# A two-layer encoder on one Trainium2 core: the middle of the first output projection as four seven-product units, and the recurrent unit in twelve turns

## The chip, the core and the metric

The kernel runs on one core of a Trainium2 chip. The metric is the device time of one execution in microseconds; the time given for a kernel is the median of its runs. The profile is of one more execution, taken with the hardware profiler. Engines carry the names of the profile: PE (TensorE), DVE (VectorE), ACT (ScalarE), POOL (GpSimd), SP (the queue that issues most transfers).

## What is computed

An encoder of two layers on 512 tokens of 2048 features, in 32-bit floats. The first layer is attention (8 query heads, 2 key heads) beside a gated linear recurrent unit of 1024 features; the second is a chunked matrix-memory recurrence. Cut to the part that the change touches, the first layer is

```
hn   = rmsnorm(x, gain)
proj = hn @ w_in                       # q, k, v, g_attn, x_lru, g_lru
attn = softmax attention of q, k, v
xc   = conv4(x_lru) + conv_b
r, i = sigmoid(xc @ wa + ba), sigmoid(xc @ wx + bx)
a    = exp(8 * r * log_sigmoid(lam))
u    = sqrt(1 - a*a) * (i * xc)
y    = scan(h = a*h + u) forward + the same backward
mix  = [attn * silu(g_attn), y * silu(g_lru)]
x    = x + mix @ w_out                 # the first output projection
```

and the second layer begins with `rmsnorm(x) @ w_in2`.

## The kernel before

**Matmuls.** Every product of two 32-bit matrices is three matmuls (`mm3`, L170; issued on L157): each operand is split into a high part (a cast on ACT, L153) and a low part (a subtraction on DVE, L154), and high by low, high by high and low by high are summed in PSUM. Activations lie with features on the partitions, 256 features (a "chunk") to a tile, so a product over 2048 features has eight steps.

**Groups and units.** The work of TensorE is a list of groups, built at the end of `build` and run by `run_steps` (L298). A plain group makes 512 output features in 8 steps, each of 24 matmuls of 128x512, into four PSUM banks (the tiles `bk`), that is 192 matmuls. A seven-product unit (`run_w7`, L396; layout "W7") makes 256 features from seven products instead of eight for each 2x2 block: 21 matmuls of 128x256 in a step, 168 in a unit (tiles `s`). For that it needs four sums of weight blocks, made on POOL (`w7_sums`, L355, tiles `w7s`; four instructions for two steps, 16 in a unit), four sums of token blocks for each chunk (`t_sums`, L544, tiles `ts`, also on POOL, made once), and the splits of both (`th`, `tl`; the unsummed parts are `bh`, `bl`). A unit takes its PSUM banks from the pool "bulk" or the pool "aux" by turns (`f` even or odd), and its result is put together from PSUM on DVE in pieces, spread over the steps of the next unit (`later`, `w7_plain`).

**What runs beside.** `ahead` (L287) loads weights (`raw`, SP) three steps ahead and splits them (`wh`, `wl`) two ahead; for units four and three. Two lanes hold generators: lane 0 statistics and attention, lane 1 the recurrent unit `lru_gen` (L847), once for each of four pairs of blocks (called LRU 0 to 3 here). A `yield` ends a turn. After every step lane 1 has one turn, and one more in the first `more` steps of a group. `mix_split(c)` (L935) multiplies nothing itself: it runs both lanes until chunk c of `mix` is finished and splits it.

**The order of groups in layer 1** is kv, Q0, L0, L1 (inputs of the recurrent unit), Q1, GL0, GL1 (its gates), GA0, GA1 (gates of attention), then four groups of the first output projection (out1), each 512 features. During GA1's steps the chunks of `mix` are split in the order 0, 1, 4, 5, 6, 7, 2, 3. The evacuation of an out1 group (`out1_evac`, L959) adds x to the result, stores the rows to memory (`x2d`), scales and splits them for layer 2 (`b_ops`, L558), stores the scaled rows (`xgd`) and adds their squares. Layer 2 then runs a plain group QK0, twelve units SQ and SZ, and further groups. The last units of the program (`LATE`) belong to the second output projection; their results are added onto the rows of `x2d` by an accumulating transfer that POOL issues (`out2_onto`, L1367).

**The recurrent unit** has 13 turns: two for the convolution, four for the gate products (`lg`, results in `lr` and `li`), one for sigmoid and tanh, one for exp (L908), the square (POOL, L911) and DVE's L912, an empty one, one for the square root (ACT, L917) and the product `ii * tau` (POOL, L918), an empty one, two for the scans (DVE, L923 and L925) and the sum y (POOL, L927).

Of the kernel before, what the change touches and what calls it, by code (L numbers as in the profile page):

```python
# [12 lines left out]
F32 = mybir.dt.float32  # L13
# [6 lines left out]
P = 128  # L20
S = 512
# [20 lines left out]
class Builder:  # L42
# [255 lines left out]
    def run_steps(self, groups):  # L298
# [5 lines left out]
        for g in groups:  # L304
# [15 lines left out]
            for c in range(NCH):  # L320
# [3 lines left out]
                for b in range(g.get("nb", 4)):  # L324
                    if c == 0:
                        g["ps"][b] = self.bank.tile([P, 512], F32, tag="bulk", name=self.name("bk"))
# [175 lines left out]
class Layer1(Builder):  # L502
# [344 lines left out]
    def lru_gen(self, i):  # L847
# [57 lines left out]
        for j in range(2):  # L905
# [3 lines left out]
            for d in range(2):  # L909
                e2 = self.half("le2")  # L910
                nc.gpsimd.tensor_tensor(out=e2, in0=rr[j][:, d, :], in1=rr[j][:, d, :], op=ALU.mult)  # L911
                v.scalar_tensor_tensor(out=tau[j][:, d, :], in0=e2, scalar=1.0, in1=tau[j][:, d, :],  # L912
                                       op0=ALU.add, op1=ALU.mult)
        yield
        yield
        for j in range(2):
            nc.scalar.activation(tau[j], tau[j], AF.Sqrt)  # L917
            nc.gpsimd.tensor_tensor(out=ii[j], in0=ii[j], in1=tau[j], op=ALU.mult)  # L918
        yield
        yield  # L920
        y = self.slot2("y")
        for j in range(2):
# [4 lines left out]
            nc.gpsimd.tensor_tensor(out=y[:, j, :], in0=tau[j][:, 0, :], in1=tau[j][:, 1, :], op=ALU.add)  # L927
# [7 lines left out]
    def mix_split(self, c):  # L935
# [4 lines left out]
        self.ms.append(self.x_ops(self.mixv.pop(c)))  # L940

    def x_ops(self, x):
        h, l = self.slot2("oh", F32R), self.slot2("ol", F32R)
        self.split(h, l, x)
        return tuple(t.rearrange("p j (t s) -> p j t s", t=2) for t in (h, l))
# [13 lines left out]
    def out1_evac(self, g):  # L959


        def evac(b, ps):
            nc, k = self.nc, 4 * g + b
            i, j = k // 2, k % 2
            x3 = self.xres[i][:, j, :]
            nc.vector.tensor_add(x3, x3, ps)
            if j == 0:
                return
            x = self.xres.pop(i)
            rows = slice(2 * i * P, (2 * i + 2) * P)  # L970
            nc.sync.dma_start(out=self.x2d[rows, :].rearrange("(j p) s -> p j s", p=P), in_=x)
            xg = self.slot2("xg")
            for j in range(2):
                k = 2 * i + j
                nc.scalar.activation(xg[:, j, :], x[:, j, :], AF.Copy, scale=self.pb[:, PB_G2 + k:PB_G2 + k + 1])
            self.x2s.append(self.b_ops(xg))
            nc.sync.dma_start(out=self.xgd[rows, :].rearrange("(j p) s -> p j s", p=P), in_=xg)
            for j in range(2):
                sq = self.half("sqx")
# [10 lines left out]
class Layer2(Layer1):  # L990
# [376 lines left out]
    def out2_onto(self, i):  # L1367

        return lambda t: self.nc.gpsimd.dma_start(out=self.rows2(self.x2d, i), in_=t, accum_op=ALU.add)
# [415 lines left out]
```

## Time and profile before

| | |
|---|---|
| three runs | 1641.71, 1645.04, 1645.58 us (median 1645.04) |
| profiled execution | 1641.33 us |
| its span on the core | 1639.6 us |
| granted TensorE clock, mean | 0.994 |
| busy: DVE, ACT, POOL | 68%, 52%, 45% |
| bytes moved | 218.12 MB, 133 GB/s |

The span is what the profile shows between first and last instruction; the execution's own time is 1.7 us more. A time of the profile is read as a position in that span. A matmul of 128x512 is shown as 0.39 us long, but the next begins 0.23 us after it, since they are pipelined: a stretch is worth its number of matmuls times this pitch, and lost time shows as a gap in PE or as a granted clock under 1.00. "Idle before" with an arrow names what ended the wait of an engine.

### The profile page before, as it was taken

The numbers are of one execution on the slowest core, as the hardware profiler recorded it, in microseconds if no ns is written. First come the engines' busy times: TensorE is split into PE (matmuls) and PEld (weight loads), VectorE is DVE, ScalarE is ACT, GpSimd is POOL, SyncE is SP. The second block draws the span as 40 slices with busy tenths as digits, with TensorE's granted clock in tenths as the row PEclk, the third lists the DMA queues.
The fourth block names the chain that finished last, engine by engine and source line by source line (L and its number), as shares of the span: only waits on it lengthen the run. The fifth ranks groups of instructions, "written<-read, shape, count | busy, mean of one in ns | idle before, by whom it ended". The sixth has DMA issues, their size and how long they took to land.

```text
span 1639.6 us, 25389 instructions
## 1 busy us (share of the span) xinstructions
PE 1610.4 (98%) x9698; PEld 1424.1 (87%) x9698; DVE 1122.1 (68%) x1714; ACT 850.1 (52%) x1395; POOL 745.6 (45%) x732
## 2 busy tenths in 40 slices
PE   9999999999989999999999999999999999999997
PEld 7888888888768888889999999999988888888997
DVE  8755476855774333457999986666777577668976
ACT  6334665667763333334445443444576466665453
POOL 5220122303130111386698778888611322368872
PEclk9999999999989999999999999999999999999999
DMA  6433133321324544644444443444554444452565
GB/s 229 134 93 98 52 103 103 92 88 52 107 71 157 178 169 155 200 140 126 121 129 138 133 142 106 129 134 134 184 168 126 129 153 142 153 182 80 142 176 176
DMA packets 138698, 218.12 MB, mean 133 GB/s; under 512 B 9792, under 2 KB 62400, under 8 KB 138576
## 3 DMA queue, kind: packets, MB, share of 16 engines
q1 hardware_dynamic: 136304, 213.80, 41.5%
q0 software_dynamic: 1088, 2.10, 0.8%
q8 instruction: 76, 1.25, 0.3%
q10 hardware_dynamic: 1184, 0.60, 0.1%
q14 instruction: 46, 0.38, 0.1%
HBM read 182.36 MB, written 34.11 MB: 132 GB/s over the span
## 4 chain that ended last, share of the span: by engine, by line
PE 83%; DVE 6%; ACT 4%; POOL 3%; issue 3%; DMA 1%; SPq 0%; DVEq 0%; POOLq 0%; ACTq 0%
PE bk L157 44%; PE s L157 29%; DVE wl L154 2%; PE nb L157 2%; PE nf L157 1%; PE PV L157 1%; PE ST L157 1%; PE lg L157 1%; PE S L157 1%; PE tr L160 1%; ACT wh L153 1%; PE gt L157 0%; DMA hTr<-hTd 0%; DVE ltau L923 0%; DVE ltau L925 0%
## 5 line engine op out<-in xcount | busy, mean ns | idle before, releaser
L154 DVE TENSOR_TENSOR wl<-raw,wh 128x1024 fp32r<-128x1024 f32 (+3 forms) x333 | 363.4, 1093 | 267.4 <-ACT wh L153 266.7
L153 ACT CAST wh<-raw 128x1024 fp32r<-128x1024 f32 (+3 forms) x333 | 265.9, 800 | 435.7 <-PE s L157 224.5
L363 POOL TENSOR_TENSOR w7s<-raw 128x256 f32<-128x256 f32 x216 | 222.5, 1048 | 95.5 <-DMA raw<-in_odd_w_in_dram 68.2
L154 DVE TENSOR_TENSOR wl<-w7s,wh 128x512 fp32r<-128x512 f32 (+1 forms) x176 | 203.7, 1158 | 6.3 <-ACT wh L153 6.3
L157 PE MATMUL bk<-xh,wl 128*128 128x512 f32 x384 | 152.1, 396 | 5.7 <-DVE wl L154 5.7
L157 PE MATMUL s<-th,wl 128*128 128x256 f32 x544 | 153.2, 282 | 0.8 <-DVE wl L154 0.8
L157 PE MATMUL s<-th,wh 128*128 128x256 f32 x544 | 152.7, 281 | 0.5 <-ACT wh L153 0.5
L157 PE MATMUL s<-tl,wh 128*128 128x256 f32 x544 | 153.0, 281 | 0.0
L157 PE MATMUL bk<-xh,wh 128*128 128x512 f32 x384 | 152.2, 396 | 0.0
L157 PE MATMUL bk<-xl,wh 128*128 128x512 f32 x384 | 152.0, 396 | 0.0
L153 ACT CAST wh<-w7s 128x512 fp32r<-128x512 f32 (+1 forms) x176 | 125.6, 714 | 17.9 <-POOL w7s L363 17.9
L363 POOL TENSOR_TENSOR w7s<-w7s,raw 128x256 f32<-128x256 f32 x108 | 120.3, 1114 | 0.0
L157 PE MATMUL s<-bh,wh 128*128 128x256 f32 x408 | 115.3, 283 | 0.9 <-ACT wh L153 0.9
L157 PE MATMUL s<-bh,wl 128*128 128x256 f32 x408 | 114.8, 281 | 0.3 <-DVE wl L154 0.3
L157 PE MATMUL s<-bl,wh 128*128 128x256 f32 x408 | 114.4, 280 | 0.0
L903 POOL TENSOR_TENSOR li<-li,xc 128x512 f32<-128x512 f32 x16 | 21.4, 1361 | 191.9 <-ACT li L895 191.9
L363 POOL TENSOR_TENSOR w7s<-raw,w7s 128x256 f32<-128x256 f32 x108 | 101.1, 936 | 7.8
L157 PEld LDWEIGHTS s<-th,wl 128*128 128x128 f32 x544 | 102.8, 189 | 1.3 <-DVE wl L154 1.3
L157 PEld LDWEIGHTS s<-th,wh 128*128 128x128 f32 x544 | 102.4, 188 | 0.7 <-ACT wh L153 0.7
L157 PEld LDWEIGHTS s<-tl,wh 128*128 128x128 f32 x544 | 102.5, 188 | 0.0
L157 PE MATMUL bk<-oh,wh 128*128 128x512 f32 x256 | 101.0, 394 | 0.0
L157 PE MATMUL bk<-ol,wh 128*128 128x512 f32 x256 | 100.8, 394 | 0.0
(349 smaller groups left out, 4532.6 us busy)
## 6 DMA issues: line engine op xcount, KB each, us to landing
raw<-in_odd_w_in_dram SPq DMA_DIRECT2D x120, 512.0 KB, 3.9
raw<-in_even_w_in_dram SPq DMA_DIRECT2D x71, 512.0 KB, 3.7
raw<-in_even_w_out_dram SPq DMA_DIRECT2D x32, 512.0 KB, 3.7
raw<-in_odd_w_out_dram SPq DMA_DIRECT2D x32, 512.0 KB, 3.7
xres<-in_xT_dram SPq DMA_DIRECT2D x8, 512.0 KB, 6.4
x2d<-xres SPq DMA_DIRECT2D x8, 512.0 KB, 4.3
xgd<-xg SPq DMA_DIRECT2D x8, 512.0 KB, 4.0
xr<-xgd SPq DMA_DIRECT2D x8, 512.0 KB, 7.3
```

Of the source, the lines that this page charges most:

```text
L153: self.nc.scalar.copy(h, x)
L154: (eng or self.nc.vector).tensor_tensor(out=l, in0=x, in1=h.bitcast(F32), op=ALU.subtract)
L157: self.nc.tensor.matmul(out, a, b, start=start, stop=stop)
L160: self.nc.tensor.transpose(out, x, ident)
L363: po.tensor_tensor(out=s[:, :, q, :], in0=x, in1=y, op=op)
L903: nc.gpsimd.tensor_tensor(out=ii[j][:, d, :], in0=ii[j][:, d, :], in1=xc[:, j, :], op=ALU.mult)
```

## The change

1. *Out1.* The groups of features 0 to 511 and 1536 to 2047 stay plain; the 1024 features between them become four seven-product units, i = 2 to 5, whose results are added onto rows of `x2d` by the accumulating transfer (`onto`). So that x is in those rows beforehand, four copies from the input to `x2d` are put on SP's queue after Q0. The chunks of `mix` are now split in the form that both layouts read (`b_ops`), and they need token sums: chunks 0 to 5 in order of their making are stored to memory (`md`) and loaded again (`mr`) during the first out1 group for the sums on POOL; the last two are summed directly. Evacuating the first group only adds and stores. In the last out1 group, whose banks are now those of "aux", chunks 0 to 5 of the new rows are loaded back (`x2_load`), one a step, and scaled, split and squared (`x2_rows`), which each group did for its own rows before.
2. *Recurrent unit.* The square goes from POOL to ACT, the product `ii * tau` from POOL to DVE, every second sum y to DVE; the empty turns go, the root, the product and the scan each have a turn: 12 turns.
3. *Extra turns.* `more` was 8 in GA0 and 0 in GA1, and is 0 in GA0 and 4 in GA1.

`rows2` and `onto` were methods of layer 2 (`out2_onto`) and are now in the shared class.

```diff
@@ -323,7 +323,8 @@
                 ws = self.wsp.pop(i)
                 for b in range(g.get("nb", 4)):
                     if c == 0:
-                        g["ps"][b] = self.bank.tile([P, 512], F32, tag="bulk", name=self.name("bk"))
+                        pool, tag = (self.aux, "aux") if g.get("aux") else (self.bank, "bulk")
+                        g["ps"][b] = pool.tile([P, 512], F32, tag=tag, name=self.name("bk"))
                     self.bulk_mm(g, g["ps"][b], g["x"](c), ws, b, c)
                     if (c < NCH - 1 or b < 1 and "turns" in g) and b in g.get("turns", (1,)):
                         self.pump(0)
@@ -908,15 +909,15 @@
                 nc.scalar.activation(rr[j][:, d, :], rr[j][:, d, :], AF.Exp, scale=self.lamn[:, c:c + 1])
             for d in range(2):
                 e2 = self.half("le2")
-                nc.gpsimd.tensor_tensor(out=e2, in0=rr[j][:, d, :], in1=rr[j][:, d, :], op=ALU.mult)
+                nc.scalar.activation(e2, rr[j][:, d, :], AF.Square)
                 v.scalar_tensor_tensor(out=tau[j][:, d, :], in0=e2, scalar=1.0, in1=tau[j][:, d, :],
                                        op0=ALU.add, op1=ALU.mult)
         yield
-        yield
         for j in range(2):
             nc.scalar.activation(tau[j], tau[j], AF.Sqrt)
-            nc.gpsimd.tensor_tensor(out=ii[j], in0=ii[j], in1=tau[j], op=ALU.mult)
-        yield
+        yield
+        for j in range(2):
+            v.tensor_mul(ii[j], ii[j], tau[j])
         yield
         y = self.slot2("y")
         for j in range(2):
@@ -924,7 +925,7 @@
                                  initial=0.0, op0=ALU.mult, op1=ALU.add)
             v.tensor_tensor_scan(out=tau[j][:, 1, ::-1], data0=rr[j][:, 1, ::-1], data1=ii[j][:, 1, ::-1],
                                  initial=0.0, op0=ALU.mult, op1=ALU.add)
-            nc.gpsimd.tensor_tensor(out=y[:, j, :], in0=tau[j][:, 0, :], in1=tau[j][:, 1, :], op=ALU.add)
+            (v if j else nc.gpsimd).tensor_tensor(out=y[:, j, :], in0=tau[j][:, 0, :], in1=tau[j][:, 1, :], op=ALU.add)
             if j == 0:
                 yield
         self.mixv[4 + i] = y
@@ -937,12 +938,25 @@
             if c not in self.mixed:
                 self.drain_until(ln, lambda: c in self.mixed or not self.lanes[ln])
         assert c in self.mixed
-        self.ms.append(self.x_ops(self.mixv.pop(c)))
-
-    def x_ops(self, x):
-        h, l = self.slot2("oh", F32R), self.slot2("ol", F32R)
-        self.split(h, l, x)
-        return tuple(t.rearrange("p j (t s) -> p j t s", t=2) for t in (h, l))
+        x, n = self.mixv.pop(c), len(self.ms)
+        self.ms.append(self.b_ops(x))
+        if n < 6:
+            self.md[n] = self.dp.tile([P, 2, S], F32, tag=f"md{n}", name=f"md{n}")
+            self.nc.sync.dma_start(out=self.md[n], in_=x)
+        else:
+            self.t_sums(n, self.ms[n], x)
+
+    def m7_load(self, c):
+        if c < 6:
+            self.xraw[c] = self.slot2("mr")
+            self.nc.sync.dma_start(out=self.xraw[c], in_=self.md[c])
+
+    def rows2(self, d, i):
+        return d[2 * i * P:(2 * i + 2) * P, :].rearrange("(j p) s -> p j s", p=P)
+
+    def onto(self, i):
+
+        return lambda t: self.nc.gpsimd.dma_start(out=self.rows2(self.x2d, i), in_=t, accum_op=ALU.add)
 
     def res_pre(self, chunks, src, first=None):
 
@@ -958,32 +972,39 @@
 
     def out1_evac(self, g):
 
-
         def evac(b, ps):
-            nc, k = self.nc, 4 * g + b
-            i, j = k // 2, k % 2
+            i, j = 2 * g + b // 2, b % 2
             x3 = self.xres[i][:, j, :]
-            nc.vector.tensor_add(x3, x3, ps)
-            if j == 0:
-                return
-            x = self.xres.pop(i)
-            rows = slice(2 * i * P, (2 * i + 2) * P)
-            nc.sync.dma_start(out=self.x2d[rows, :].rearrange("(j p) s -> p j s", p=P), in_=x)
-            xg = self.slot2("xg")
-            for j in range(2):
-                k = 2 * i + j
-                nc.scalar.activation(xg[:, j, :], x[:, j, :], AF.Copy, scale=self.pb[:, PB_G2 + k:PB_G2 + k + 1])
-            self.x2s.append(self.b_ops(xg))
-            nc.sync.dma_start(out=self.xgd[rows, :].rearrange("(j p) s -> p j s", p=P), in_=xg)
-            for j in range(2):
-                sq = self.half("sqx")
-                nc.scalar.activation(sq, x[:, j, :], AF.Square)
-                if i == 0 and j == 0:
-                    self.acc = self.half("acc")
-                    nc.gpsimd.tensor_copy(self.acc, sq)
-                else:
-                    nc.gpsimd.tensor_tensor(out=self.acc, in0=self.acc, in1=sq, op=ALU.add)
+            self.nc.vector.tensor_add(x3, x3, ps)
+            if j:
+                x = self.xres.pop(i)
+                self.nc.sync.dma_start(out=self.rows2(self.x2d, i), in_=x)
+                if g:
+                    self.x2_rows(i, x)
         return evac
+
+    def x2_load(self, c):
+        if 0 < c < 7:
+            self.xraw[c - 1] = self.slot2("x2r")
+            self.nc.sync.dma_start(out=self.xraw[c - 1], in_=self.rows2(self.x2d, c - 1))
+
+    def x2_rows(self, i, x):
+
+        nc = self.nc
+        xg = self.slot2("xg")
+        for j in range(2):
+            k = 2 * i + j
+            nc.scalar.activation(xg[:, j, :], x[:, j, :], AF.Copy, scale=self.pb[:, PB_G2 + k:PB_G2 + k + 1])
+        self.x2s[i] = self.b_ops(xg)
+        nc.sync.dma_start(out=self.rows2(self.xgd, i), in_=xg)
+        for j in range(2):
+            sq = self.half("sqx")
+            nc.scalar.activation(sq, x[:, j, :], AF.Square)
+            if i == 0 and j == 0:
+                self.acc = self.half("acc")
+                nc.gpsimd.tensor_copy(self.acc, sq)
+            else:
+                nc.gpsimd.tensor_tensor(out=self.acc, in0=self.acc, in1=sq, op=ALU.add)
 
 
 
...
@@ -1575,7 +1589,10 @@
             return tuple(t.rearrange("p (t j) s -> p j t s", t=2) for t in self.hs[c]["B"])
 
         x1 = self.x1s.__getitem__
-        mx = self.ms.__getitem__
+
+        def mx(c):
+            return tuple(t.rearrange("p (t j) s -> p j t s", t=2) for t in self.ms[c]["B"])
+
         add = self.add
         groups = [grp(w1, 1024, "tok", x1, self.kv_evac, pre=kv_pre, ld=self.x_load(a["xT"]),
                       first=lambda: self.x_parts(0, self.x1s), mid=lambda: self.stats(),
@@ -1585,6 +1602,9 @@
             def f():
                 add(0, self.q_gen(g))
                 add(0, self.attn_gen(g))
+                if g == 0:
+                    for i in range(2, 6):
+                        self.nc.sync.dma_start(out=self.x2d[256 * i:256 * i + 256, :], in_=a["xT"][256 * i:256 * i + 256, :])
             return f
 
         def after_lru(g):
@@ -1595,7 +1615,7 @@
 
         L = [grp(w1, 2560 + 512 * g, "T", x1, self.xlru_evac(g), after=after_lru(g)) for g in range(2)]
         Q = [grp(w1, 512 * g, "tok", x1, self.q_evac(g), after=after_q(g)) for g in range(2)]
-        GA = [grp(w1, 1536 + 512 * g, "T", x1, self.gate_evac(2 * g), more=8 - 8 * g) for g in range(2)]
+        GA = [grp(w1, 1536 + 512 * g, "T", x1, self.gate_evac(2 * g), more=4 * g) for g in range(2)]
         GL = [grp(w1, 3584 + 512 * g, "T", x1, self.gate_evac(4 + 2 * g)) for g in range(2)]
         groups += [Q[0], L[0], L[1], Q[1], GL[0], GL[1], GA[0], GA[1]]
 
@@ -1612,10 +1632,22 @@
         def late(c):
             if c >= 6:
                 mix_next()
+            else:
+                self.t_sums(c, self.ms[c], self.xraw.pop(c))
+
+        def again(c):
+            if c >= 2:
+                self.x2_rows(c - 2, self.xraw.pop(c - 2))
+
+        def out1(g, pre, ld, **kw):
+            return grp(wo1, 512 * g, "T", mx, self.out1_evac(g), order=order, ld=ld,
+                       pre=self.res_pre((2 * g, 2 * g + 1), a["xT"], pre), **kw)
 
         groups[-1]["pre"] = early
-        groups += [grp(wo1, 512 * g, "T", mx, self.out1_evac(g), order=order,
-                       pre=self.res_pre((2 * g, 2 * g + 1), a["xT"], None if g else late)) for g in range(4)]
+        groups += [out1(0, late, self.m7_load)]
+        groups += [dict(w=wo1[:, 256 * i:256 * i + 256], lay="W7", f=i - 1, order=order, x=self.ms.__getitem__,
+                        evac=self.onto(i)) for i in range(2, 6)]
+        groups += [out1(3, again, self.x2_load, aux=True)]
 
         QK0 = grp(w2, 0, "T", x2, self.qk_evac(0), wqk=(0, 1024), pre=qk_pre, ld=self.x7_load)
 
@@ -1681,7 +1713,7 @@
             return dict(w=wo2[:, 256 * i:256 * i + 256], lay="W7", f=i + 1, order=range(NCH), x=self.hs.__getitem__,
                         evac=evac, **kw)
 
-        groups += [u7(i, self.out2_onto(i)) for i in LATE]
+        groups += [u7(i, self.onto(i)) for i in LATE]
         groups.append(u7(6, self.out2_7(6), pre=self.res_pre((6,), self.x2d),
                          each=late_rows))
         groups.append(dict(w=wo2[:, 1792:2048], lay="last", order=range(NCH), pre=self.res_pre((7,), self.x2d)))
```

How the instructions move, at the three places that matter later. DVE, round the third step of GA1, before: `wl_3851` is the low part of that step's weights, `li_3550` and `lr_3549` belong to LRU 3, `ol` are low parts of mixed chunks (a scan is listed as a scalar_tensor_tensor).

```order
L832 TENSOR_TENSOR mixr_3803<-mixr_3803,gate_3810 128x1024
L154 TENSOR_TENSOR ptl_3816<-tr_3817,pth_3815 128x4x128
L912 SCALAR_TENSOR_TENSOR ltau_3710<-le_3768,ltau_3710 128x512
L923 SCALAR_TENSOR_TENSOR ltau_3709<-lr_3549,li_3550 128x512
L925 SCALAR_TENSOR_TENSOR ltau_3709<-lr_3549,li_3550 128x512
L154 TENSOR_TENSOR ol_3847<-mixr_3801,oh_3846 128x1024
L154 TENSOR_TENSOR wl_3851<-raw_3771,wh_3850 128x1024
L154 TENSOR_TENSOR ptl_3816<-tr_3868,pth_3815 128x4x128
L154 TENSOR_TENSOR ol_3892<-mixr_3803,oh_3891 128x1024
```

The weight's low part stands behind the first two scans, which read what POOL's L918 made. DVE after the change, the same stretch: `wl_3958` belongs to the weights of GA1's fifth step (those of the third and fourth stand ahead of these rows), `bl` are low parts of mixed chunks.

```order
L154 TENSOR_TENSOR bl_3882<-mixr_3759,bh_3881 128x2x2x256
L913 SCALAR_TENSOR_TENSOR ltau_3869<-le_3899,ltau_3869 128x512
L913 SCALAR_TENSOR_TENSOR ltau_3869<-le_3902,ltau_3869 128x512
L913 SCALAR_TENSOR_TENSOR ltau_3870<-le_3907,ltau_3870 128x512
L913 SCALAR_TENSOR_TENSOR ltau_3870<-le_3910,ltau_3870 128x512
L920 TENSOR_TENSOR li_3658<-li_3658,ltau_3869 128x1024
L920 TENSOR_TENSOR li_3795<-li_3795,ltau_3870 128x1024
L154 TENSOR_TENSOR bl_3952<-mixr_2709,bh_3951 128x2x2x256
L154 TENSOR_TENSOR wl_3958<-raw_3879,wh_3957 128x1024
L924 SCALAR_TENSOR_TENSOR ltau_3869<-lr_3657,li_3658 128x512
L926 SCALAR_TENSOR_TENSOR ltau_3869<-lr_3657,li_3658 128x512
L154 TENSOR_TENSOR wl_4000<-raw_3949,wh_3999 128x1024
```

The products `li` times `ltau` are now here (L920), and the scans (L924, L926) stand behind them and behind the weight of the fifth step. POOL, from LRU 3 to the first squares of layer 2's rows, before:

```order
L903 TENSOR_TENSOR li_3550<-li_3550,xc_3459 128x512 x2
L903 TENSOR_TENSOR li_3620<-li_3620,xc_3459 128x512 x2
L911 TENSOR_TENSOR le_3757<-lr_3549 128x512
L911 TENSOR_TENSOR le_3760<-lr_3549 128x512
L911 TENSOR_TENSOR le_3765<-lr_3619 128x512
L911 TENSOR_TENSOR le_3768<-lr_3619 128x512
L918 TENSOR_TENSOR li_3550<-li_3550,ltau_3709 128x1024
L918 TENSOR_TENSOR li_3620<-li_3620,ltau_3710 128x1024
L927 TENSOR_TENSOR y_3939<-ltau_3709 128x512
L927 TENSOR_TENSOR y_3939<-ltau_3710 128x512
L983 COPY acc_4428<-sqx_4426 128x512
L985 TENSOR_TENSOR acc_4428<-acc_4428,sqx_4430 128x512
```

The whole recurrent part stands there, and no token or weight sum. After the change the same engine has, from the second of the four new units to the third:

```order
L364 TENSOR_TENSOR w7s_4793<-raw_4791 128x2x128 x2
L364 TENSOR_TENSOR w7s_4793<-w7s_4793,raw_4791 128x2x128
L364 TENSOR_TENSOR w7s_4793<-raw_4791,w7s_4793 128x2x128
L364 TENSOR_TENSOR w7s_4864<-raw_4862 128x2x128 x2
L364 TENSOR_TENSOR w7s_4864<-w7s_4864,raw_4862 128x2x128
L364 TENSOR_TENSOR w7s_4864<-raw_4862,w7s_4864 128x2x128
L959 DMA x2d<-x_4829 128x2x512
L364 TENSOR_TENSOR w7s_4930<-raw_4928 128x2x128 x2
L364 TENSOR_TENSOR w7s_4930<-w7s_4930,raw_4928 128x2x128
L364 TENSOR_TENSOR w7s_4930<-raw_4928,w7s_4930 128x2x128
```

Four instructions (three rows, one of them x2) make the sums of two steps' weights. The accumulating transfer of the first unit's result (L959, `x_4829`) stands between the last sums of the second unit and the first of the third; the squares L911 and the products L918 have gone from this queue.

More of the change, by code (lines that the diff above doesn't have):

```diff
@@ L914, in lru_gen @@
         yield
+        for j in range(2):
+            nc.scalar.activation(tau[j], tau[j], AF.Sqrt)
         yield
         for j in range(2):
-            nc.scalar.activation(tau[j], tau[j], AF.Sqrt)
-            nc.gpsimd.tensor_tensor(out=ii[j], in0=ii[j], in1=tau[j], op=ALU.mult)
-        yield
+            v.tensor_mul(ii[j], ii[j], tau[j])
         yield
@@ L1365, in out2_evac @@
             self.x3_store(b // 2)
-    def out2_onto(self, i):
-        return lambda t: self.nc.gpsimd.dma_start(out=self.rows2(self.x2d, i), in_=t, accum_op=ALU.add)
     def out2_7(self, i):
@@ L1377, in out2_7 @@
         return lambda t: self.later.extend(partial(part, t, j) for j in range(2))
-    def rows2(self, d, i):
-        return d[2 * i * P:(2 * i + 2) * P, :].rearrange("(j p) s -> p j s", p=P)
     def x3_load(self, i):
@@ L1543, in build @@
         self.gate_done, self.value_done, self.mixed = set(), set(), set()
-        self.xres, self.xraw, self.x1s, self.x2s, self.ms, self.hs = {}, {}, [], [], [], []
+        self.xres, self.xraw, self.x1s, self.x2s, self.ms, self.hs, self.md = {}, {}, [], {}, [], [], {}
         self.qk, self.v2, self.hfb = {}, {}, {}
```

## The prediction

> **What bounds the kernel now.** I read the page first: the engines' shares and the granted clock.
>
> ```profile
> span 1639.6 us, 25389 instructions
> PE 1610.4 (98%) x9698; PEld 1424.1 (87%) x9698; DVE 1122.1 (68%) x1714; ACT 850.1 (52%) x1395; POOL 745.6 (45%) x732
> PEclk9999999999989999999999999999999999999999
> ```
>
> TensorE is busy for 98% of the span. So time is won in two ways only: fewer matmul cycles, or the few places where TensorE stands or runs at a lower clock. One slice of the clock row, the twelfth (451 to 492 us), shows an 8 among the nines, so I asked next for the list of TensorE's waits.
>
> ```profile
> PE bk L157 <- DVE wl L154: 6.4, 2, 5.7
> PE s L157 <- ACT wh L153: 1.7, 3, 0.9
> PE s L157 <- DVE wl L154: 1.1, 3, 0.5
> ```
>
> The columns are total, times and longest, in us. The largest (5.7) is a 512-feature group waiting for a weight's low part from VectorE. The rows named s are the seven-product units, and there is hardly any wait in them. The third view is the windows: first the four groups of the first output projection, then two stretches of seven-product units that the kernel has already, then the two places round the long waits. Columns: window, its length, busy us (instructions) of PE, PEld, DVE, ACT, POOL, then granted clock, DMA share, GB/s.
>
> ```profile
> 513.00:691.00 178.00, 178.00 (x770) 144.29 (x769) 67.83 (x61) 59.78 (x74) 27.20 (x23) 1.00 0.50 165
> 910.00:950.00 40.00, 40.00 (x342) 39.80 (x341) 36.58 (x55) 19.73 (x37) 31.22 (x33) 1.00 0.45 131
> 1510.00:1600.00 90.00, 89.68 (x755) 89.48 (x756) 77.11 (x107) 45.80 (x88) 70.20 (x72) 1.00 0.59 167
> 410.00:420.00 10.00, 6.33 (x30) 4.99 (x29) 8.67 (x12) 5.72 (x9) 2.20 (x2) 0.86 0.26 63
> 420.00:425.00 5.00, 5.00 (x22) 3.94 (x21) 5.00 (x8) 2.89 (x7) 0.00 (x0) 0.94 0.51 149
> 460.00:470.00 10.00, 9.01 (x42) 6.99 (x41) 4.32 (x5) 9.94 (x13) 5.00 (x4) 1.00 0.00 0
> 470.00:475.00 5.00, 1.15 (x5) 0.62 (x5) 5.00 (x4) 3.57 (x4) 2.66 (x2) 0.68 0.00 0
> 475.00:480.00 5.00, 3.14 (x11) 2.85 (x12) 5.00 (x5) 0.00 (x0) 0.72 (x1) 0.50 0.38 104
> 480.00:485.00 5.00, 5.00 (x21) 4.16 (x20) 5.00 (x5) 3.21 (x4) 0.73 (x1) 0.79 0.57 176
> ```
>
> The output projection runs without a gap at full clock, and so do the units. Round 415 and 475 us TensorE idles, and afterwards runs slowly for some us.
>
> **The change part by part.** *A, two groups become four units.* A group is 192 matmuls of 128x512; by the first window one takes 178.00/770 = 0.2312 us, so two groups take 384 x 0.2312 = 88.8 us. A unit is 168 matmuls of 128x256. In the last units of the program, whose result GpSimd also adds onto rows in memory, one takes 90.00/755 = 0.1192 us, a unit 20.0, four units 80.1: **-8.7 us**. Bounds: at the pace of the second window (40.00/342 = 0.1170, 19.65 a unit) -10.2; with one wait of 0.5 in each unit (the longest of the s rows on VectorE) 20.5 a unit, -6.7. I take the middle, because those units do just what the new ones do.
>
> The cover of a unit is GpSimd's weight sums, 16 an eight-step unit, and one accumulating DMA:
>
> ```profile
> L363 POOL TENSOR_TENSOR w7s<-raw 128x256 f32<-128x256 f32 x36 | 35.1, 994 | 12.6 <-DMA raw<-in_odd_w_out_dram 7.6 <-ACT wh L153 4.9
> L363 POOL TENSOR_TENSOR w7s<-w7s,raw 128x256 f32<-128x256 f32 x18 | 19.3, 1072 | 0.0
> L363 POOL TENSOR_TENSOR w7s<-raw,w7s 128x256 f32<-128x256 f32 x19 | 17.4, 916 | 1.4
> L1369 POOL DMA_DIRECT2D x2d<-x x4 | 5.0, 1254 | 0.3
> L363 POOL TENSOR_TENSOR w7s<-w7s,raw 128x256 f32<-128x256 f32 x1 | 1.7, 1710 | 0.0
> DMA to landing us min/median/max: 6.0/6.4/10.2
> ```
>
> (The first four rows are from 1500 to 1600 us; the fifth, from 696 to 727 us, is one sum that ran beside a busy VectorE; the last is the accumulating DMAs' time to landing.) That is 8 x 0.994 + 4 x 1.072 + 4 x 0.916 = 15.9, with the DMA 17.2 of 20.0 us: covered, with 2.8 us to spare. VectorE had 36.58 of 40 us in the second window and kept up. That VectorE's and GpSimd's times hang together shows in the fifth row (1.71 against 1.07 as the mean). [...]
>
> The rows that were two groups' scaling, splitting and squares (chunks 0 to 5 now) move into the last group. In the first window 32 casts and subtracts of weights and eight chunks' work took VectorE 67.83 and ScalarE 59.78 us. A group keeps 8 of the 32 (a quarter of about 33 us on ScalarE, of about 39 on VectorE), so it holds at most 8 + 27 = 35 us on ScalarE, 10 + 29 = 39 on VectorE, of 44.4: hidden, **0**. Its reloads stand on SP's queue behind the accumulation that they read; the last is asked for in the group's fourth step, some 16 us after the last accumulation is issued, against 10.2 at most to landing. Weight loads queue behind it on SP, so 6 us of lateness there would show.
>
> *B, the way into the first unit.* The unit's loads run one step further ahead than a group's and need their sums first. The same turn out of the second output projection's group showed:
>
> ```profile
> PE s L157 <- ACT wh L153: 1.4, 2, 0.9
> PE s L157 <- DVE wl L154: 0.6, 2, 0.3
> ```
>
> That is 2.0 us between 1499 and 1515; from 740 to 772 us, where the QK group passes into units, the list of TensorE's waits is empty. Bounds 0 and +2.0; I take **+1.0**. The mixed chunks' token sums, 4 operations a chunk, lie in the first out1 group, where GpSimd has nothing else.
>
> *C, the recurrent unit.* What the two places cost: idle 3.67 us at 410 to 420, and at lower clock 6.33 x 0.14 + 5.00 x 0.06 = 1.2, together 4.9; idle 0.99 + 3.85 + 1.86 = 6.7 at 460 to 480, and clock 1.15 x 0.32 + 3.14 x 0.50 + 5.00 x 0.21 = 3.0, together 9.7. In all 14.6 us. [...] What makes the second wait, in the timelines of GpSimd, VectorE and TensorE:
>
> ```profile
> 466.55 4.74 POOL L918 TENSOR_TENSOR li<-li,ltau 128x1024 f32<-128x1024 f32 x2 [2.01 <-ACT ltau L917]
> 468.98 3.39 DVE L923 TENSOR_TENSOR_SCAN ltau<-lr,li 128x512 f32<-128x512 f32 x1 [3.72 <-POOL li L918]
> 472.29 1.19 DVE L925 TENSOR_TENSOR_SCAN ltau<-lr,li 128x512 f32<-128x512 f32 x1
> 473.41 1.19 DVE L154 TENSOR_TENSOR ol<-mixr,oh 128x1024 fp32r<-128x1024 f32 x1
> 474.52 2.28 DVE L154 TENSOR_TENSOR wl<-raw,wh 128x1024 fp32r<-128x1024 f32 x1
> 476.86 0.80 PE L157 MATMUL bk<-xh,wl 128*128 128x512 f32 x1 [5.71 <-DVE wl L154]
> ```
>
> VectorE stands 3.72 us for GpSimd's product, its first scan takes 3.39 beside GpSimd instead of 1.19, and the weights of GA1's third step stand behind that. In the changed order the products are on VectorE, the squares on ScalarE, and the weights of GA1's fourth step stand ahead of the whole chain; those of the fifth stand behind the products. From the square root to the end of the weight's low part it was 476.80 - 466.55 = 10.25 us; now it is two products, one low part and the weight's: 2 x 1.22 + 1.21 + 1.29 = 4.9. So the wait of 5.7 goes if the rest of the chain is no later. What is late next: ScalarE's row up to the cast of that fifth weight, with these durations:
>
> ```profile
> L153 ACT CAST wh<-raw 128x1024 fp32r<-128x1024 f32 x14 | 14.7, 1047 | 18.1 <-PE bk L157 15.6 <-DMA raw<-in_even_w_in_dram 2.5
> L810 ACT ACTIVATE gate<-gate 128x512 f32<-128x512 f32 x8 | 5.0, 630 | 2.7 <-DVE gate L809 2.6
> L908 ACT ACT_TABLE_LOAD x3 | 3.8, 1283 | 0.0
> L908 ACT ACTIVATE lr<-lr,lamn 128x512 f32<-128x512 f32 x4 | 2.9, 722 | 0.0
> L895 ACT ACTIVATE lr<-lr 128x1024 f32<-128x1024 f32 x2 | 2.1, 1062 | 0.0
> L671 ACT ACTIVATE sqt<-qraw 128x512 f32<-128x512 f32 x4 | 2.5, 635 | 0.1
> L832 DVE TENSOR_TENSOR mixr<-mixr,gate 128x1024 f32<-128x1024 f32 x4 | 4.9, 1220 | 0.2
> L154 DVE TENSOR_TENSOR wl<-raw,wh 128x1024 fp32r<-128x1024 f32 x14 | 18.1, 1294 | 13.1 <-ACT wh L153 13.1
> ```
>
> From the end of GA0's products on, its row holds five table loads (6.4), two of the four sigmoids (2.1), tanh and exp, eight (5.8), four squares (2.5, by the squares of the queries), two roots (2.1), five casts (5.2) and eight short ones of the gates and attention (at most 0.37 to 0.63 each, some 4): 28 us if nothing overlaps what came before, and the low part ends 1.3 to 2.5 us later, at about 29 to 30. TensorE reaches the fifth step after 4 x 24 x 0.2312 = 22.2 us of the group, 3.5 of attention (455.5 to 471.15 held two steps, 0.99 of wait and 3.5 of that) and 2.8 of the recurrent gates' 12 matmuls: 28.5. So a wait of about 1 us there, as much near LRU 2, too short for the clock to fall: 2.5 us of the 14.6 stay, **-12.0**. Bounds: none stays, -14.6; all comes back, 0. On GpSimd nothing waits for the moved products: its queue there is short (5.00 of 10 us at 460). ScalarE's added squares are in the sum above.
>
> *D, copies and stores.* Four copies of 0.52 MB from input to rows stand early on SP's queue, two ahead of one weight load and two ahead of the next, where ScalarE already waits for weights:
>
> ```profile
> 48.23 1.05 ACT L153 CAST wh<-raw 128x1024 fp32r<-128x1024 f32 x1 [3.84 <-DMA raw<-in_even_w_in_dram]
> q1 hardware_dynamic: 136304, 213.80, 41.5%
> ```
>
> 213.80 MB took 41.5% of 1639.6 us, or 0.314 MB/us; a copy is then 1.7 us, two are 3.4, in steps of 5.6 with weights split two ahead. Bounds 0 and +3.4; I take **+0.5**, nearer to none, since TensorE shows no wait for ScalarE's weight there. Six stores and reloads of mixed chunks come to 6 MB more in the half-loaded window of 0.50: 0.
>
> The sum: -8.7 + 1.0 - 12.0 + 0.5 = -19.2. The profiled execution took 1641.33 us, so 1622.1. The three runs have their median at 1645.04; the four executions lie in two pairs (1641.33 and 1641.71, 1645.04 and 1645.58), whose mean is 1643.4. From there: **1624 us**.
>
> **The rivals.** *The wait comes back one place on.* The whole chain of LRU 3, from its gates' products, runs some 24 us later, and ScalarE's row has no slack by my own working. If it is 4 us longer than I count, the fifth step waits as the third did, clock and all: +7.2 (9.7 less what I left), 1631; for it stands ScalarE's 9.94 of 10 us at 460 to 470, against it the 10.25 us that shrink to 4.9. [...] *The recurrent part brings nothing*, because ScalarE was the true limit: +12, 1636. *Slower: GpSimd becomes the bound of the units.* Its 17.2 of 20.0 us leaves 2.8; if its 16 sums take over 1.17 us each, it sets the pace, and it eats everything from (88.8 + 10.5 - 5.0)/4 = 23.6 us a unit, that is 1.40 us a sum; to be slower by 4.9 it must take (88.8 + 10.5 + 4.9)/4 = 26.1, or 1.55 a sum. At the 1.71 of the row above it would be 28.6 us a unit, 4 x 8.6 = +34, 1658. For it: 36.58 of 40 us of VectorE beside GpSimd are in the units at 910, and sums there may be longer. Against it: with those very shares the unit took 19.65.
>
> **How the numbers follow.** Forecast 0.58; the wait one place on 0.20; slower units 0.10; no gain in the recurrent part 0.07; GpSimd the bound 0.05. A measurement of this kernel can tell 0.3%, 4.9 us, from no change; faster means under 1640.1. All but the last of the cases lie under it by themselves; where two of them come together (1624 + 7 + 9) they reach 1640, for which I put 0.07 on the same. So faster 0.88, same 0.07, slower 0.05. The range goes down to 1614 (A and C at their best, 1643.4 - 10.2 - 14.6 = 1618.6, and the lower pair of executions 2 us under the mean, with 2 for what I can't see), and up to 1637, past the third rival; two joined rivals and the slower one are left out.
>
> **What would show it.** In the changed trace: the stretch from the first out1 group to the QK group about 9 us shorter and without gaps, units of 19.7 to 20.5 us, GpSimd's sums at 0.9 to 1.1; no wait over 2 us of a group on wl between 400 and 510, and no clock under 0.9 in that stretch. It is wrong if TensorE waits there for a wl or wh over 3 us, if GpSimd's sums pass 1.2 us, or if a raw or x2r transfer holds TensorE.

## The result and the profile after

The changed kernel takes 1619.29 us (median of 4 runs, 1618.26 to 1620.87) against 1645.31 before (4 runs, 1641.71 to 1649.20): a ratio of 0.9842, 95% interval 0.9818 to 0.9866, or 26.0 us less. Between the two profiled executions (1641.33 and 1620.87) it is 20.5. The page after:

```profile
span 1619.1 us, 26278 instructions
PE 1598.5 (99%) x9986; PEld 1431.9 (88%) x9986; DVE 1172.1 (72%) x1802; ACT 881.8 (54%) x1470; POOL 802.7 (50%) x804
PEclk9999999999999999999999999999999999999998
```

The slice at 451 to 492 us, an 8 before, is a 9 now; the last slice, a 9 before, is an 8. From the list of TensorE's waits after (total, times, longest):

```profile
PE stc L157 <- DVE acc L1435: 2.5, 1, 2.5
PE s L157 <- DVE wl L154: 2.4, 5, 0.8
PE rB L157 <- DVE diag L601: 2.2, 1, 2.2
...
PE S L157 <- ACT attn L775: 1.1, 1, 1.1
...
PE bk L157 <- DVE wl L154: 0.7, 1, 0.7
```

The 5.7 of a group on wl is gone (the 0.7 left lies in the first 60 us). The longest waits that are left, stc and rB, lie in the final norm, which the change does not touch. The windows, in the columns of the prediction: the first out1 group, the four units, the last out1 group, then the recurrent part up to out1.

```profile
498.70:543.20 44.50, 44.50 (x193) 36.09 (x192) 31.89 (x26) 17.69 (x23) 40.49 (x37) 1.00 0.46 167
543.20:622.00 78.80, 78.80 (x666) 78.78 (x665) 63.42 (x83) 36.70 (x68) 55.92 (x58) 1.00 0.56 156
622.00:668.00 46.00, 46.00 (x204) 37.48 (x203) 25.99 (x24) 27.30 (x38) 26.61 (x21) 1.00 0.84 264
380.00:400.00 20.00, 18.63 (x93) 15.05 (x93) 15.94 (x24) 19.83 (x29) 0.00 (x0) 1.00 0.08 26
400.00:425.00 25.00, 25.00 (x127) 20.86 (x127) 20.10 (x33) 15.94 (x27) 2.12 (x1) 1.00 0.59 190
425.00:460.00 35.00, 35.00 (x173) 29.11 (x172) 21.64 (x31) 26.08 (x37) 2.56 (x3) 1.00 0.37 121
460.00:485.00 25.00, 25.00 (x116) 20.58 (x115) 19.10 (x18) 18.64 (x23) 6.86 (x5) 1.00 0.25 85
```

From 400 us to the second layer TensorE is busy throughout (one wait of 0.3 us is listed), at a clock of 1.00. Three positions in the two traces show where the time came from. The first matmul of out1 starts at 498.7 instead of 513.1 (14.4 earlier); out1 lasts 168.7 instead of 178.0 (9.3 less); the 3.2 us by which the 20.5 falls short of the sum of 23.7 were lost behind it (out1's end to the first matmul of the last group 912.1 instead of 911.3, from there to the squares' sum 15.2 instead of 13.6, the rest 24.5 instead of 23.6), where no instruction has changed.

### The profile page after: what moved, and what is told of

The parts are those of the page before. It is cut to its first block, busy times and chain, and to the rows that moved or that the text cites. A ratio compares the mean times of both kernels' runs of the same rounds, so it can differ in the third digit from the quotient of the medians.

```text
span 1619.1 us, 26278 instructions
## 1 busy us (share of the span) xinstructions
PE 1598.5 (99%) x9986; PEld 1431.9 (88%) x9986; DVE 1172.1 (72%) x1802; ACT 881.8 (54%) x1470; POOL 802.7 (50%) x804
## 4 chain that ended last, share of the span: by engine, by line
PE 86%; DVE 4%; ACT 4%; POOL 2%; issue 2%; DMA 2%; SPq 0%; DVEq 0%; ACTq 0%; POOLq 0%
PE bk L157 41%; PE s L157 34%; DVE wl L154 2%; PE nf L157 2%; PE nb L157 2%; PE lg L157 1%; PE PV L157 1%; PE ST L157 1%; PE S L157 1%; PE tr L160 1%; ACT wh L153 1%; PE gt L157 0%; DMA hTr<-hTd 0%; DMA xres<-x2d 0%; DMA raw<-in_odd_w_out_dram 0%
## 5 line engine op out<-in xcount | busy, mean ns | idle before, releaser
L154 DVE TENSOR_TENSOR wl<-raw,wh 128x384 fp32r<-128x384 f32 (+3 forms) x349 | 365.4, 1049 | 185.0 <-ACT wh L153 184.3
L153 ACT CAST wh<-raw 128x384 fp32r<-128x384 f32 (+3 forms) x349 | 265.0, 762 | 378.8 <-PE s L157 274.9
L364 POOL TENSOR_TENSOR w7s<-raw 128x256 f32<-128x256 f32 x248 | 252.0, 1035 | 107.2 <-DMA raw<-in_odd_w_in_dram 61.4
L154 DVE TENSOR_TENSOR wl<-w7s,wh 128x512 fp32r<-128x512 f32 (+1 forms) x208 | 237.1, 1140 | 4.4 <-ACT wh L153 4.3
L157 PE MATMUL s<-th,wl 128*128 128x256 f32 x672 | 190.2, 283 | 0.8 <-DVE wl L154 0.8
L157 PE MATMUL s<-th,wh 128*128 128x256 f32 x672 | 189.1, 281 | 0.5 <-ACT wh L153 0.5
L157 PE MATMUL s<-tl,wh 128*128 128x256 f32 x672 | 189.2, 282 | 0.0
L157 PE MATMUL bk<-bh,wh 128*128 128x512 f32 (+1 forms) x352 | 136.2, 387 | 0.0
L157 PE MATMUL bk<-bh,wl 128*128 128x512 f32 (+1 forms) x352 | 135.2, 384 | 0.0
L157 PE MATMUL bk<-bl,wh 128*128 128x512 f32 (+1 forms) x352 | 135.1, 384 | 0.0
```

The costliest lines, as they stand in the source:

```text
L153: self.nc.scalar.copy(h, x)
L154: (eng or self.nc.vector).tensor_tensor(out=l, in0=x, in1=h.bitcast(F32), op=ALU.subtract)
L157: self.nc.tensor.matmul(out, a, b, start=start, stop=stop)
L364: po.tensor_tensor(out=s[:, :, q, :], in0=x, in1=y, op=op)
```

## The experiments

Positions in each kernel's profiled execution, and the medians (the kernel before ran again beside the others, with medians of 1645.0 to 1645.7):

| kernel | start of out1 | length of out1 | median us |
|---|---|---|---|
| before | 513.1 | 178.0 | 1645.3 |
| changed | 498.7 | 168.7 | 1619.3 |
| changed, again | 498.6 | 168.7 | 1620.8 |
| recurrent part alone | 498.5 | 178.2 | 1631.4 |
| units alone | 512.6 | 168.6 | 1633.9 |
| product alone | 500.1 | 178.1 | 1632.8 |
| units and product | 500.4 | 168.7 | 1622.0 |
| product on GpSimd | 511.0 | 169.1 | 1632.6 |
| old extra turns | 505.6 | 168.5 | 1629.1 |
| square on GpSimd | 498.9 | 168.7 | 1622.5 |
| copies later | 498.9 | 169.2 | 1620.5 |
| half more sums | 499.1 | 182.9 | 1632.3 |

**Do the two parts add up?** First the recurrent part alone, with the kernel before's four plain groups.

```diff
+ lru_gen of the changed kernel
+ more=4 * g in GA
  four plain out1 groups
```

> The four plain groups of the first output projection as before; only the recurrent unit in 12 turns and the extra turns moved (0 and 4). Theory (the two parts are separate and add up): the change took 14.4 us before the first output projection and 9.2 in it, so this kernel should take 14 to 17 us less than before, about 1629, with no wait of a group for wl over 1 us and no clock under 0.95 between 400 and 510 us. Rival (the units are what matters, the stall would have gone with them): 1640 and more, with a wait near 475 us still there.

Measured 1631.37 (1629.66 to 1632.91), ratio 0.9919 [0.9907, 0.9932], 14.0 us under before; out1 starts at 498.5, and the longest wait of a group for wl is 0.7. Then the units alone.

```diff
+ four units, copies, stores and reloads
  lru_gen with 13 turns
  more=8 - 8 * g in GA
```

> The four units, the copies, the stores and reloads as changed; the recurrent unit in 13 turns and extra turns 8 and 0 as before. Theory: first output projection 169 us instead of 178, the two stalls at 410 to 425 and 460 to 485 us as before (about 14 us lost there), the time 9 to 10 us under before, about 1636. Rival (the stall depends on what the mixed chunks' splits and stores put on the same engines): the loss there grows or shrinks by over 4 us, and the time differs from 1636 by as much.

Measured 1633.89 (1632.12 to 1635.10), ratio 0.9934 [0.9920, 0.9947], 11.4 us under before, a little more than the 9 to 10 expected. Its two longest waits, to the digit those of the kernel before:

```profile
PE bk L157 <- DVE wl L154: 6.4, 2, 5.7
PE PV L157 <- DVE ptl L154: 2.9, 2, 2.7
```

14.0 and 11.4 are 25.4, against 26.0 for both. So the two parts add up, and the stall does not go with the units.

**Which line of the recurrent part?** The changed kernel with the product of gate and root put back on GpSimd:

```diff
-            v.tensor_mul(ii[j], ii[j], tau[j])
+            nc.gpsimd.tensor_tensor(out=ii[j], in0=ii[j], in1=tau[j], op=ALU.mult)
```

> The changed kernel with one thing undone: the product of gate and root is on GpSimd again, in its turn. Theory (GpSimd's product between root and scan is what made the weights late): a wait of a group for wl of 3 to 6 us comes back in GA1 or GL1, and the time is 4 to 10 us over the changed kernel's 1619, at 1623 to 1629. Rival (the shift of turns and the square on ScalarE did it): within 2 us of the changed kernel, no wait over 1 us.

Measured 1632.61 (1630.69 to 1634.51), 13 us over the changed kernel: more than the 4 to 10 expected, and about all that the recurrent part had brought. GpSimd and VectorE in GA1:

```profile
477.33 4.78 POOL L920 TENSOR_TENSOR li<-li,ltau 128x1024 f32<-128x1024 f32 x2 [7.60 <-ACT ltau L917]
```

```profile
479.78 3.42 DVE L924 TENSOR_TENSOR_SCAN ltau<-lr,li 128x512 f32<-128x512 f32 x1 [4.42 <-POOL li L920]
483.12 1.20 DVE L926 TENSOR_TENSOR_SCAN ltau<-lr,li 128x512 f32<-128x512 f32 x1
485.35 2.28 DVE L154 TENSOR_TENSOR wl<-raw,wh 128x1024 fp32r<-128x1024 f32 x1
```

The picture of before is back, one place on: VectorE stands 4.42 us for GpSimd, the scan beside it takes 3.42, and the weights stand behind; TensorE waits 3.2 us here and 2.5 near 405, and 3.1 at 227, a third place, where neither the kernel before nor the changed one has a wait. The reverse, that line alone in the kernel before:

```diff
  13 turns, more=8 - 8 * g, four plain groups
-            nc.gpsimd.tensor_tensor(out=ii[j], in0=ii[j], in1=tau[j], op=ALU.mult)
+            v.tensor_mul(ii[j], ii[j], tau[j])
```

> The kernel before with one line changed: the product of gate and root on VectorE; still 13 turns, the square on GpSimd, extra turns 8 and 0, four plain groups. Theory (GpSimd's product between root and scan is the whole cause of the two stalls): 12 to 14 us under before, about 1632, no wait of a group for wl over 1.5 us between 400 and 490 us. Rival (the product is one of two causes, the place of the turns the other): half of it, 5 to 9 us under before, with a wait of 2 to 4 us left near 475 us.

Measured 1632.78 (1631.86 to 1633.91), ratio 0.9927 [0.9914, 0.9940], 12.2 under before. VectorE, at the place of the 5.7 us wait:

```profile
461.69 2.36 DVE L918 TENSOR_TENSOR li<-li,ltau 128x1024 f32<-128x1024 f32 x2 [1.24 <-ACT ltau L917]
463.97 1.22 DVE L154 TENSOR_TENSOR ol<-mixr,oh 128x1024 fp32r<-128x1024 f32 x1
465.11 1.22 DVE L154 TENSOR_TENSOR wl<-raw,wh 128x1024 fp32r<-128x1024 f32 x1
```

Both products take 2.36 us there, where GpSimd took 4.74, and the scans no longer stand ahead of the weights; between 60 and 700 us no wait for a wl is left. One line holds nearly the whole worth of the recurrent part. With the units it should then give the changed kernel's time:

```diff
  four units as changed
  13 turns, more=8 - 8 * g, product on VectorE
```

> The four units as changed, and of the recurrent part only the product on VectorE: 13 turns, square and sums y on GpSimd, extra turns 8 and 0. Theory (that line is the whole worth of the recurrent part; turns, squares and extra turns add nothing by themselves): within 2 us of the changed kernel. Rival (the units need the shorter chain, since the mixed chunks are stored and loaded again behind it): 3 to 8 us over it, with a wait in GA1 or in the first out1 group.

Measured 1622.04 (1620.23 to 1624.51), ratio to before 0.9857 [0.9844, 0.9871]. The changed kernel itself ran on the same chip, as the measure for this and the next two:

> The changed kernel once more, unchanged, as the measure for the other three on the same chip: 1618 to 1621, and in the trace no wait over 1.5 us between 400 and 670 us.

It gave 1620.76 (1618.16 to 1623.72), ratio 0.9849 [0.9835, 0.9862], with 1.1 us as its longest wait between 60 and 700 us. The two can't be told apart by time; in the traces out1 starts 1.8 us later without the other edits. The square by itself:

```diff
-                nc.scalar.activation(e2, rr[j][:, d, :], AF.Square)
+                nc.gpsimd.tensor_tensor(out=e2, in0=rr[j][:, d, :], in1=rr[j][:, d, :], op=ALU.mult)
```

> The changed kernel with the square of the recurrent unit on GpSimd again, the product still on VectorE. Theory (each GpSimd operation in the chain costs its 1.0 us and a handover, four of them partly beside exp, against 1.8 us that the fifth step of GA1 had to spare): a wait of 0 to 2 us, the time 0 to 4 us over the changed kernel. Rival (any operation of GpSimd in this chain brings the stalls back): 8 us and more over it.

Measured 1622.50 (1620.96 to 1624.06), ratio 0.9859 [0.9845, 0.9872]: no difference that can be measured, and out1 starts at 498.9. GpSimd in the chain is no stall as such; GpSimd between the last root and the scans was (13 us over the changed kernel, above).

**Are the moved extra turns idle?**

```diff
-        GA = [... more=4 * g) for g in range(2)]
+        GA = [... more=8 - 8 * g) for g in range(2)]
```

> The changed kernel with the extra turns as before (8 in GA0, 0 in GA1). Theory (the product alone counts): within 2 us of the changed kernel, 1617 to 1621. Rival (the later place of LRU 3's chain is needed as well): a wait of 2 us and more in GA1's first steps, 1623 to 1629.

Measured 1629.06 (1626.12 to 1630.62), 9.8 us over the changed kernel: the theory failed, and the rival had the place right and the size nearly (1623 to 1629). It is GA1's first matmul that waits; what it waits for is not a weight but a gate's evacuation, and the clock is lower there. With both, out1 starts 6.9 us later:

```profile
PE bk L157 <- DVE gate L810: 3.6, 1, 3.6
```

```profile
440.00:460.00 20.00, 16.37 (x78) 13.36 (x77) 17.49 (x23) 18.66 (x28) 2.01 (x1) 0.89 0.31 106
460.00:470.00 10.00, 10.00 (x46) 8.27 (x45) 8.15 (x9) 4.76 (x6) 0.00 (x0) 0.87 0.56 210
```

VectorE at the border of GA0 and GA1 in that kernel:

```profile
452.39 1.20 DVE L924 TENSOR_TENSOR_SCAN ltau<-lr,li 128x512 f32<-128x512 f32 x1
453.51 2.22 DVE L926 TENSOR_TENSOR_SCAN ltau<-lr,li 128x512 f32<-128x512 f32 x1
455.66 1.19 DVE L154 TENSOR_TENSOR wl<-raw,wh 128x1024 fp32r<-128x1024 f32 x1
456.77 2.47 DVE L810 TENSOR_TENSOR gate<-bk,rB 128x512 f32<-128x512 f32 x4
```

The matmul starts at 457.50. With 12 turns and the old extra turns LRU 3's scans come to the very end of GA0, ahead of the evacuation (L810) that must free GA0's banks before GA1's first matmul. So the extra turns were moved for the 12 turns' sake: 13 turns with the old ones (units and product, above) and 12 turns with the new ones are both without a stall, 12 with the old ones are not.

**How near is GpSimd to the bound of a unit?** Two of four weight sums are computed twice in the new units:

```diff
-            po.tensor_tensor(out=s[:, :, q, :], in0=x, in1=y, op=op)
+            for _ in range(2 if twice and q % 2 == 0 else 1):
+                po.tensor_tensor(out=s[:, :, q, :], in0=x, in1=y, op=op)
```

> The changed kernel, with two of the four weight sums of each pair of steps computed twice in the four new units (same result): 24 instead of 16 instructions of GpSimd a unit. Theory (GpSimd covers its work with some 3 us a unit to spare and sets the pace beyond that): a unit's GpSimd time is 16 x 0.96 + 8 x 0.89 + 1.26 = 23.7 us against 19.7 of TensorE, so the four units become about 95 instead of 79 us less what runs ahead, and the time 12 to 17 us longer, 1631 to 1636, with TensorE waiting for wh in the units. Rival (sums that run four steps ahead take it up, or the sums get shorter when they no longer wait for VectorE): under 5 us longer.

Measured 1632.30 (1631.34 to 1633.98), 13 us over the changed kernel, as expected. GpSimd from 543 to 640 us in it, and TensorE's two largest sums of waits from 490 to 700 (on wl, where waits for wh were expected):

```profile
L365 POOL TENSOR_TENSOR w7s<-raw 128x256 f32<-128x256 f32 x56 | 53.4, 1007 | 1.0 <-DVE wl L154 1.0
L365 POOL TENSOR_TENSOR w7s<-w7s,raw 128x256 f32<-128x256 f32 x14 | 14.2, 1015 | 0.0
```

```profile
PE s L157 <- DVE wl L154: 5.0, 5, 2.8
PE bk L157 <- DVE wl L154: 1.9, 3, 1.0
```

GpSimd has hardly any idle time left before a sum (1.0 us in all before 56 of them), and out1 takes 182.9 instead of 168.7. In the changed kernel, from 543 to 622 us, the rows were:

```profile
L364 POOL TENSOR_TENSOR w7s<-raw 128x256 f32<-128x256 f32 x26 | 22.5, 888 | 9.5 <-DMA raw<-in_even_w_out_dram 6.8 <-DVE wl L154 1.6 <-DVE w7u L489 1.0
L364 POOL TENSOR_TENSOR w7s<-w7s,raw 128x256 f32<-128x256 f32 x13 | 14.2, 1096 | 0.0
L364 POOL TENSOR_TENSOR w7s<-raw,w7s 128x256 f32<-128x256 f32 x14 | 13.9, 994 | 1.1
L959 POOL DMA_DIRECT2D x2d<-x x3 | 3.8, 1260 | 2.6 <-DVE x L498 2.6
```

So a unit takes GpSimd 8 x 0.888 + 4 x 1.096 + 4 x 0.994 + 1.26 = 16.7 of 19.7 us in the changed kernel. In the run above its 24 sums of about 1.0 us pass the length of a unit, and TensorE is held up; the slower case of the prediction only had its condition unmet in the changed kernel.

**The copies.**

```diff
-                if g == 0:
+                if g == 1:
                     for i in range(2, 6):
                         self.nc.sync.dma_start(out=self.x2d[...], in_=a["xT"][...])
```

> The changed kernel with the four copies from input to rows put on SP's queue after Q1 instead of Q0. Theory (where they stand they cost TensorE nothing): within 1.5 us of the changed kernel. Rival (they delay weights at 45 us by up to 3.4 us): 1 to 3 us under it, with less time lost in the first 100 us.

Measured 1620.53 (1619.03 to 1621.67), ratio 0.9848 [0.9835, 0.9862], the changed kernel's own (0.9849): they cost no more where they stand than behind Q1.

**A version that goes on from here.** The wait for the last sum of squares (2.5 us) has the same shape, GpSimd between two operations of VectorE:

```diff
-            (self.nc.gpsimd if 4 <= k < 14 else self.nc.vector).tensor_tensor(
+            (self.nc.gpsimd if 4 <= k < 12 else self.nc.vector).tensor_tensor(
```

> The changed kernel with the last two additions of squares of the final norm (feature tiles 12 and 13) on VectorE instead of GpSimd. Theory (as in the recurrent unit, an operation of GpSimd between two of VectorE costs its own time and the handover): TensorE's wait of 2.5 us for these squares at the end shrinks to under 1, the time 1 to 2 us under the changed kernel, about 1618. Rival (VectorE is as late by itself there): no difference.

Measured 1618.89 (1616.42 to 1622.69), ratio 0.9844 [0.9825, 0.9863]: not to be told from the changed kernel. The wait was 1.3 us in its trace. But it was 1.4 in that of the later copies, where nothing at that place differs, and 0.9 to 3.1 in the others, so its trace does not settle it either.

**The kernel before once more.**

> The kernel before, unchanged, for a second profile. The runs differ by 26 us in their medians, the two profiled executions by 20.5. Theory (the stalls of the kernel before vary between executions, since what follows a wait is a lower clock): the loss between 400 and 490 us is not 14.6 but up to 20 here. Rival: the same 14 to 15 us there, and the rest of the difference is spread over the program.

Its one execution took 1641.86, with the same waits (5.7 and 2.7) and out1 at 513.6: the loss is 0.5 us larger, not the 5 of the theory. Only the time at a lower clock differs: 0.72 from 410 to 420 us, where the prediction's row has 0.86. What differs between executions is the mean granted clock: 0.990 to 0.994 in the runs of the kernel before (1641.8 to 1648.1 us) and 0.991 to 0.994 in those of the units alone, both with the stalls; 0.995 to 0.998 in all runs of the kernels without long waits (the changed one, the recurrent part alone, the product alone with and without the units, the square, the copies, the last squares). 0.004 of 1640 us is 6.6 us, about the size of the gap of 5.5 between 26.0 by medians and 20.5 by the profiles. Both profiles of the kernel before are of its quicker executions (0.994 and 0.993); where the clock was lower in the slower ones no trace shows, and that stays open. But the traces do show that such stretches come and go between executions of one kernel, at places that the change does not touch. The first row is the kernel before again, the other two are the first and the second profile of the changed kernel:

```profile
410.00:420.00 10.00, 6.31 (x27) 5.14 (x26) 8.67 (x13) 6.02 (x9) 1.90 (x2) 0.72 0.28 76
1480.00:1490.00 10.00, 8.30 (x52) 7.50 (x51) 8.60 (x15) 8.60 (x16) 5.06 (x7) 0.83 0.43 157
1480.00:1490.00 10.00, 8.71 (x67) 7.89 (x66) 8.59 (x14) 9.44 (x18) 5.12 (x6) 1.00 0.50 175
```

Both profiles of the changed kernel have four short waits there (1.7 and 1.3 us in all), and the clock falls in one of them. Nor does the length of a single wait decide it: with the product on GpSimd the 3.1 us at 227 us leave the clock at 1.00 (225 to 235 us), and the 2.5 us near 405, a shorter wait, stand beside 0.72 (406 to 412 us).

## Why the prediction held, step by step

*A, the units.* Forecast -8.7, measured -9.3 (178.0 to 168.7), near the bound of the faster window: 19.7 us a unit, at the pace of 910 to 950 us and not of the last units. The length of out1 holds B and the last group's added rows too, and those were hidden as forecast (ScalarE 27.30 and VectorE 25.99 of 46.00 us). VectorE and GpSimd together show 63.42 + 55.92 us of work in 78.80, so at least 40 us of it overlap as listed. Slower units, for which the prediction has a chance of 0.10 and the 9 us where two cases come together, no run of the changed kernel shows: out1 took 168.7 us in both of its traces.

*B, the way in.* Forecast +1.0, measured 0: TensorE has no wait at all between 543 and 670 us. GpSimd was less free in the first group than I wrote (40.49 of 44.50 us, with the token sums), and still the first unit was on time.

*C, the recurrent part.* The mechanism was right, the size too small: -12.0 forecast, -14.4 measured together with D. The step that failed is the 2.5 us that I left for two waits of about 1 us, at GA1's fifth step and near LRU 2; neither is there. That they would be too short for the clock to fall was an estimate too, which no run shows at these places: the changed kernel has 1.00 from 380 to 485 us, and its longest wait there is one of 1.1 us for attn, at 390. ScalarE and VectorE at the fifth step:

```profile
468.90 2.01 ACT L917 ACTIVATE ltau<-ltau 128x1024 f32<-128x1024 f32 x2
470.82 1.03 ACT L153 CAST bh<-mixr 128x1024 fp32r<-128x1024 f32 x1
471.76 2.94 ACT L153 CAST wh<-raw 128x1024 fp32r<-128x1024 f32 x3
```

```profile
470.07 2.36 DVE L920 TENSOR_TENSOR li<-li,ltau 128x1024 f32<-128x1024 f32 x2 [1.93 <-ACT ltau L917]
472.34 1.22 DVE L154 TENSOR_TENSOR bl<-mixr,bh 128x1024 fp32r<-128x1024 f32 x1
473.48 1.22 DVE L154 TENSOR_TENSOR wl<-raw,wh 128x1024 fp32r<-128x1024 f32 x1
474.61 1.22 DVE L924 TENSOR_TENSOR_SCAN ltau<-lr,li 128x512 f32<-128x512 f32 x1
```

From the first product to the end of the weight's low part it is 474.70 - 470.07 = 4.6 us (4.9 forecast, 10.25 before). GA1's first matmul starts at 451.1 and its fifth step at 476.6, so the low part is 1.9 us early. Counted from 451.1, ScalarE's cast ends at 21.7 us and not at 28, and the fifth step comes at 25.5 and not at 28.5: in both I put work behind GA0's end that lay ahead of it. ScalarE's error (6 us) was larger than TensorE's (3), so a wait was forecast where there is a small reserve. The rival that the wait comes back one place on fell by these 1.9 us. The experiment with the old extra turns shows how near it was, though at a border that I had not considered, the evacuation of GA0.

I also took the edits of the recurrent part as one. The product alone carries it (12.2 of 14.0 us). The square adds nothing that can be measured, the sums y were not tried by themselves, and the moved extra turns repair what the 12 turns would do. All edits but the product together put out1 1.5 to 1.8 us earlier in the traces.

*D, the copies.* Forecast +0.5, measured next to nothing: out1 starts at 498.7 with them and at 498.5 in the recurrent part alone, which has none.

*The sum.* -19.2 forecast; -23.7 at the end of out1, -20.5 over the profiled executions, -26.0 by medians. At the end of out1 the terms account for the difference of 4.5 us: 0.6 from A, 1.0 from B, 2.9 from C and D. By medians the gain was 6.8 us larger than the sum; the other 2.3 are in no term, and go with the executions above. The range held the time (1619.3 in 1614 to 1637, the upper end past the 1636 of a recurrent part that brings nothing), near the 1618.6 of A and C at their best. That the likeliest value was only 4.7 us too high is in part luck: I started from 1643.4, and the median before was 1645.3. Of the 3.2 us lost behind out1 in the first profile of the changed kernel, 0.6 is left in its second (span 1616.4). There the stretch from out1's end to the last group takes 909.8 us instead of 912.1, with the clock of 1.00 near 1480 us shown above. What lies behind it is as long in both (39.7 and 39.3 us, 37.2 before), with a clock of 0.83 from 1590 to 1600 us in both and a wait for the squares of 2.5 and 2.1 us, against a clock of 1.00 there and 0.9 us before; why, no run here shows.

## What to carry to other kernels

Where the step behind it is already late, an operation on another engine between two steps of a chain costs its own time, the wait of the engine that has the next step, and everything that stands behind that step in the order: here two products of 2.4 us on GpSimd, in each of two places, cost TensorE 12 us, the lower clock behind the waits (0.50 from 475 to 480 us) among it, though GpSimd was busy for only 9.11 of 25.00 us round the second (460 to 485 us). The squares on the same engine, earlier in the same chain, cost nothing that could be measured. Shortening such a chain moves it, and it has to be looked at again where it lands: the same scans were harmless inside a group and cost 10 us at its border, ahead of an evacuation. A seven-product unit in place of half a plain group was worth what its pitch in the trace said, as long as the engine that makes its sums kept its 3 us of 20 (16.7 of 19.7 us busy here).

## What the runs showed that I had not expected

A kernel with two waits of 2.7 and 5.7 us ran at a mean granted clock of 0.990 to 0.994, and the same program without them at 0.995 to 0.998, while the two profiles with the waits show a lower clock for only 3 to 7 us at the first and some 10 us at the second (counted as time at 0.50, the clock of 475 to 480 us). The gain by medians was larger by 5.5 us than the gain between the two profiles, which fits the lower clock of the other executions but is not traced. The last out1 group moved 264 GB/s at a DMA share of 0.84 (no fortieth of the span had over 229 GB/s before), and TensorE did not wait there, though ScalarE did (6.7 us for the reloaded rows, 6.1 for weights).
